# Later modulation columns in a fused encoder block: loads placed behind an attention output's store, products a unit later

## Chip, core and metric

One Trainium2 chip, one of its cores. The metric is device time of one execution, in microseconds (us); the median of three runs of the kernel before is 2392.31 us (2392.06 to 2393.08). All arithmetic that matters here is in 32-bit floats; matrix products are made of three passes over a rounded high part and its remainder.

## What is computed

One encoder layer on 1024 positions of width 1024. Its modulation vector is a small product that is wanted late in the layer:

```python
mod = (silu(c) @ ada_w + ada_b)                 # 1024 x 6144
shift_m, scale_m, gate_m, shift_f, scale_f, gate_f = split(mod, 6)
h = rmsnorm(x, pre_norm_mix) * (1 + scale_m) + shift_m
...                                              # h @ w_in: latents, gates, SSD inputs
y_a = sparse_mla_attention(...) @ w_o_attn       # 16 heads, top 256 keys, biases of relative position
y_b = ssd_mixer(...) @ w_o_ssd
x = x + gate_m * rmsnorm((sig(g_a) * y_a + sig(g_b) * y_b) @ w_out, post_norm_mix)
...                                              # SwiGLU with shift_f, scale_f, gate_f
```

The first 2048 columns of `mod` (shift_m, scale_m) are made at the start by TensorE. The other 4096, in 32 columns of tiles numbered 16 to 47, aren't needed until the attention is over, and are the subject here.

## The kernel before

The layer runs in stages: the normed input and its first projections, the index scores and the choice of keys (to about 668 us), the attention with the last input projections beside it (to about 1145 us), the SSD scan, the output projections, the feed-forward part.

**The attention** is 32 units: 8 pairs of heads (hp), and in each pair the four blocks of 256 queries in the order 0, 2, 1, 3. A call of `attention` weaves two things, unit by unit: the scores of this unit (`att_scores`) and the output of the one before (`att_out`).

- Scores: TensorE forms the query (`puq`, L226), ScalarE and VectorE split it into `qh` and `ql` (L803, L804), TensorE multiplies it with the keys into `plg` (L832). VectorE adds a bias and takes the minimum in one pass (L841); for the near keys the bias is `nm`, which GpSimd has made as the position's bias plus the mask (L816, twice a unit). ScalarE takes the exponential (L844), VectorE the reciprocal `rr` of its sum (L845).
- Output: GpSimd spreads `rr` into `r2` (L852), TensorE transposes the weights (`pt`, L865), ScalarE and VectorE copy them out (`pc`, L870, L868), TensorE multiplies with the values into `po` (L884), VectorE scales into `rb` (L888), and SP stores `rb` to DRAM (L889).

For the first three pairs (12 units) the projections of three last groups of the SSD inputs are woven in, one 128-row product a unit: SP loads weights `wraw` (L150), ScalarE rounds them to `whi` (L151), GpSimd takes the rest `wlo` (L152), TensorE multiplies into a bank `pw` (L236), VectorE convolves and so frees the bank (L961 to L963). `weight_sums` also loads four tiles `wsum` a unit (L997), which VectorE adds (L1002) and SP stores (L1003). In this part TensorE keeps the written order. From the fourth pair on nothing is woven in.

**The later modulation columns.** `ada_next` is called once after each projection (12 times) and once after each unit from the fourth pair on (20 times, and once for the tail). One call makes one column j: `ada_slow` has SP load two tiles `adaw` of 256 KB (L326), GpSimd multiply each by silu(c) (L327) and add the two (L329), and VectorE sum the result into a column of `adas` (L330). There are two `adaw` tiles, so the next column's loads wait until this one's sum is done. After four columns `ada_cols` sums over partitions with four one-column products on TensorE (L296), and VectorE adds the bias into `mod` (L297); it is called at j % 4 == 2.

**What sets the order.** A scheduler with a timeline model of its own places each instruction on its engine; each engine and the SP queue then run strictly in that order. `behind(instruction, first)` forbids the scheduler to place an instruction ahead of another on the same engine; without a second argument, that other one is an early instruction of the start. So before the change the loads, products and additions of a column may stand anywhere after the start.

Of the kernel before, what the change touches and what calls it, by code (L numbers as in the profile page):

```python
# [14 lines left out]
OP = mybir.AluOpType  # L15
AX = mybir.AxisListType

P = 128
# [48 lines left out]
def build(tc, a, dbg=None, stop=99, slots=None):  # L67
    nc = tc.nc
    V, S, G, T, SP = nc.vector, nc.scalar, nc.gpsimd, nc.tensor, nc.sync
# [132 lines left out]
    d_att = dr.tile([KT, P, L], F32, name="d_att")  # L202
# [115 lines left out]
        V.tensor_tensor(mod[:, k:k + 9:8], p[:, 0:2], vec[:, k:k + 9:8], op=OP.add)  # L318
        V.scalar_tensor_tensor(amul[:, k:k + 1], mod[:, 8 + k:9 + k], 1.0, col("pre_mix", k), op0=OP.add, op1=OP.mult)

    def ada_slow(j, acc):

        ts = []
        for h in range(2):
            t = wp.tile([P, 4, P], F32, name="adaw", tag="adaw", bufs=2)
            behind(SP.dma_start(t, a["ada_w"][j - 16][:, 4 * h:4 * h + 4]))  # L326
            behind(G.tensor_tensor(t, t, cs[:, 4 * h:4 * h + 4, None].to_broadcast([P, 4, P]), op=OP.mult))  # L327
            ts.append(t)
        G.tensor_tensor(ts[0], ts[0], ts[1], op=OP.add)  # L329
        V.tensor_reduce(acc, ts[0].rearrange("p k m -> p m k"), axis=AX.X, op=OP.add)  # L330

# [464 lines left out]
    def att_scores(u, uq, nb, out):  # L796

        pq = bank("puq")
        for hh in range(2):
            dense([(pq[:, 256 * hh:256 * hh + 256], u // 2, slice(256 * (u % 2), 256 * (u % 2) + 256))],  # L800
                  [(uq, 2 * hh, [0, 1])], QN)
        qh, ql = Q("qh", dt=F32R), Q("ql", dt=F32R)
        S.activation(qh, pq, AF.Copy, scale=qscale)  # L803
        V.scalar_tensor_tensor(ql, pq, qscale, f(qh), op0=OP.mult, op1=OP.subtract)  # L804
        QQ = (qh, ql)
        rr = sm.tile([P, 4], F32, name="rr", bufs=4)
        out["rr"] = rr
        yield
        for t in range(2):
            i = 2 * u + t  # L810
            n = (i + 1) * P
            near = max(0, n - 256)
            nw = n - near
            nm = Q("nm", (P, 2, 256))
            mk = MK[i][:, near:n] if i in MK else dmask[:, 256 - nw:256]
            G.tensor_tensor(nm[:, :, 0:nw], nb[:, :, 256 - nw:256], mk[:, None, :].to_broadcast([P, 2, nw]), op=OP.add)  # L816
            a_ = max(256, n - 512) if n > 512 else 0
            for hh in range(2):
                st = [QQ[x][:, 256 * hh + 128 * t:256 * hh + 128 * t + 128] for x in range(2)]
                if u >= 2:  # L820
                    lg = R("lg")
                else:
                    if hh == 0:
                        pair = R("lg")
                    lg = pair[:, half(hh)]
                mx = sm.tile([P, 4], F32, name="mx", bufs=6)
                pb_ = {}
                for o_, w_ in ((a_, n - a_),) + (((0, a_),) if a_ else ()):
                    p = bank("plg")
                    w2 = max(w_, 256)  # L830
                    for x, (qi, ki) in enumerate(P3):
                        T.matmul(p[:, 0:w2], st[qi], KVT[ki][:, o_:o_ + w2], start=x == 0, stop=x == 2)  # L832
                    pb_[o_] = p
                parts = [(a_, near, n, nm[:, hh, 0:nw])]
                if near > a_:
                    parts.append((a_, a_, near, MK[i][:, a_:near]))
                if a_:
                    parts.append((0, 0, a_, MK[i][:, 0:a_]))
                m = 3e38
                for x, (o_, s_, e_, add) in enumerate(parts):  # L840
                    V.tensor_tensor_reduce(lg[:, s_:e_], pb_[o_][:, s_ - o_:e_ - o_], add, op0=OP.add, op1=OP.min,  # L841
                                           scale=-1.0, scalar=m, accum_out=mx[:, x:x + 1])
                    m = mx[:, x:x + 1]
                S.activation(lg[:, 0:n], lg[:, 0:n], AF.Exp, scale=-1.0, bias=m, accum_out=mx[:, 3:4])  # L844
                V.reciprocal(rr[:, 2 * t + hh:2 * t + hh + 1], mx[:, 3:4])  # L845
                out[hh, t] = lg
                yield

    def att_out(hp, u, vt, PR):

        r2 = sm.tile([P, 2, 2, 64], F32, name="r2", bufs=1)
        G.tensor_copy(r2, PR["rr"].rearrange("p (t h) -> p t h", t=2)[:, :, :, None].to_broadcast([P, 2, 2, 64]))  # L852
        po = bank("po")
        pov = po[:, 0:256].rearrange("p (t n) -> p t n", t=2)
        last = 2 * u + 1
        parts, copied = {}, []

        def turn(j):
            ts = (0, 1) if j < last else (1,)
            sl = slice(ts[0], 2)  # L860
            pt = (bank if hp < HP_FIRST else bank_d)("pt")
            ptv = pt.rearrange("p (h t n) -> p h t n", h=2, t=2)
            for hh in range(2):
                for t in ts:
                    T.transpose(ptv[:, hh, t, :], PR[hh, t][:, j * P:(j + 1) * P], ident)  # L865
            pc = Q("pc").rearrange("p (h t n) -> p h t n", h=2, t=2)
            if j % 2:
                i = V.tensor_copy(pc[:, :, sl], ptv[:, :, sl])  # L868
            else:
                i = S.activation(pc[:, :, sl], ptv[:, :, sl], AF.Copy)  # L870
            parts[j] = pc, sl
            if hp >= HP_FIRST:
                copied.append(i.ins.name)

        for j in range(last + 1):
            turn(j)
            yield
        after = copied[-1] if copied else None
        for t in range(2):
            behind(T.transpose(po[:, 256 + 128 * t:384 + 128 * t], r2[:, t].rearrange("p h n -> p (h n)"), ident), after)  # L880
        for j in range(last + 1):
            pc, sl = parts.pop(j)
            for hh in range(2):
                behind(T.matmul(pov[64 * hh:64 * hh + 64, sl], vt[:, j, 64 * hh:64 * hh + 64], pc[:, hh, sl],  # L884
                                start=j == 0, stop=j == last, skip_group_check=True), after)
        rb = sm.tile([P, 256], F32, name="rb", bufs=1)
        S.activation(rb, po[:, 256:512], AF.Copy)
        V.tensor_tensor(rb, po[:, 0:256], rb, op=OP.mult)  # L888
        SP.dma_start(d_att[hp][:, 256 * u:256 * u + 256], rb)  # L889
        yield  # L890

    def weave(x, nx, y, ny, z=iter(()), nz=0, lead=1):
# [22 lines left out]
    att = {}  # L915
# [51 lines left out]

    slow, sums = iter(range(16, 48)), {}

    def ada_next():  # L970

        j = next(slow, None)
        if sums and (j is None or j % 4 == 2):
            ada_cols(*sums.popitem())
        if j is not None:
            if j % 4 == 0:
                first[j] = EV("adas", (P, 4, P))
            acc = first[j - j % 4]
            ada_slow(j, acc[:, j % 4])
            if j % 4 == 3:  # L980
                sums[j - 3] = acc

    def group(g):
        return (16 + g, d_bc[g, 0]), (24 + g, d_bc[g, 1]), (2 * g, d_xs[2 * g]), (2 * g + 1, d_xs[2 * g + 1])
# [957 lines left out]
```

## Time and profile before

| what | us |
|---|---|
| median of three runs | 2392.31 |
| the profiled execution, its own time | 2391.81 |
| span of its trace | 2389.7 |
| mean granted TensorE clock | 0.992 of full |
| TensorE busy, of the span | 2329.6 |
| GpSimd (POOL) busy, of the span | 1116.7 |
| attention, first query product to last output's store | 668 to 1144 |
| `adaw` loads: first issue, last issue | 41.0, 1058.1 |
| products with silu(c) (L327): 64, in all | 67.8 |

The page gives busy time by engine, and the costliest groups of instructions with the idle time ahead of them and what ended it. A row of waits says which engine and line waited, for what, how long in all, how often, and the longest. A row of a timeline gives start, duration, engine, line and tile, and in brackets the idle time just before and its releaser. PE is TensorE, DVE is VectorE, ACT is ScalarE, POOL is GpSimd, SPq is SP's queue of DMA issues. Rows of stretches give busy time of each engine in it (PE, PEld, DVE, ACT, POOL, with counts), then the granted clock (PEclk), the DMA share and GB/s.

### The profile page before, as it was taken

The page shows a single profiled execution, that of the slowest core. Times are in us where ns is not written, and L with a number is a line of the kernel's source. Part 1 is how long each engine was busy: PE and PEld are TensorE (multiplying, and loading weights), DVE is VectorE, ACT ScalarE, POOL GpSimd, SP SyncE. Part 2 cuts the span into 40 slices and gives each one's busy share as a digit, 9 for nine tenths or more (in the row PEclk, how much of TensorE's full clock was granted, in tenths as well). Part 3 has the DMA queues.
Part 4 walks back from the last instruction along what each step waited for, and adds up shares of the span by engine and source line. Part 5 has one row for each costly group of instructions (what it writes and reads, how often), then busy time and mean ns, then how long its engine had stood idle before and what let it go on. Part 6 is the DMA issues. An engine that isn't in the chain of part 4 may idle for free. (4 is left out here: it accounts for less than half of the span.)

```text
span 2389.7 us, 35459 instructions
## 1 busy us (share of the span) xinstructions
PE 2329.6 (97%) x11834; PEld 1897.0 (79%) x11834; DVE 1645.0 (69%) x3147; ACT 1266.8 (53%) x2440; POOL 1116.7 (47%) x872
## 2 busy tenths in 40 slices
PE   8999999999999999999999999999999999999997
PEld 6888888888887787777776777788787888888877
DVE  4566775599667676766477878475677877547776
ACT  4456665577455555545677666655564222335452
POOL 3321112222353454652245544778677555544465
PEclk9999999999999999999999999999999999999999
DMA  7123122522235553321588987766475555328664
GB/s 285 62 90 124 63 74 76 163 93 98 92 108 196 171 189 102 102 94 57 186 248 262 313 268 241 239 207 224 134 247 170 178 197 183 114 97 303 219 217 160
DMA packets 245830, 397.13 MB, mean 166 GB/s; under 512 B 24416, under 2 KB 92688, under 8 KB 245648
## 3 DMA queue, kind: packets, MB, share of 16 engines
q1 hardware_dynamic: 244352, 393.25, 49.6%
q8 instruction: 93, 1.52, 0.3%
q10 hardware_dynamic: 1296, 1.63, 0.2%
q14 instruction: 89, 0.73, 0.1%
HBM read 288.33 MB, written 109.60 MB: 167 GB/s over the span
## 5 line engine op out<-in xcount | busy, mean ns | idle before, releaser
L152 POOL TENSOR_TENSOR wlo<-wraw,whi 128x512 fp32r<-128x512 f32 x146 | 198.0, 1357 | 487.2 <-ACT whi L151 445.7
L1551 PE MATMUL p<-xh,wr 128*128 128x512 f32 x880 | 275.7, 391 | 3.8 <-DVE g L1611 2.8
L247 POOL TENSOR_TENSOR wlo<-wraw,whi 128x512 fp32r<-128x512 f32 x119 | 170.7, 1437 | 104.1 <-ACT whi L246 98.9
L1545 POOL TENSOR_TENSOR wr<-a,wr 128x512 fp32r<-128x512 f32 x110 | 159.6, 1460 | 115.0 <-ACT wr L1544 84.5
L1551 PEld LDWEIGHTS p<-xh,wr 128*128 128x128 f32 x880 | 166.0, 189 | 40.0 <-DVE g L1611 3.2
L1551 PE MATMUL p<-xl,wr 128*128 128x512 f32 x440 | 171.9, 391 | 0.0
L151 ACT ACTIVATE whi<-wraw 128x512 fp32r<-128x512 f32 x146 | 91.4, 627 | 131.1 <-issue 47.8
L844 ACT ACTIVATE lg<-lg,mx 128x256 f32<-128x256 f32 (+7 forms) x128 | 98.6, 771 | 104.8 <-DVE mx L841 101.4
L1544 ACT ACTIVATE wr<-a 128x512 fp32r<-128x512 f32 x110 | 68.7, 629 | 141.3 <-PE p L1551 118.2
L1551 PE MATMUL p<-h2h,wr 128*128 128x512 f32 x352 | 111.1, 390 | 0.0
L704 ACT ACTIVATE junk<-acc,cand__2213 128x1024 bf16<-128x1024 f32 (+2 forms) x96 | 86.2, 898 | 45.1 <-DVE cand__2213 L747 29.0
L327 POOL TENSOR_TENSOR adaw<-adaw,cs 128x512 f32<-128x512 f32 x64 | 67.8, 1061 | 88.5 <-DMA adaw<-ada_w 78.6
L246 ACT ACTIVATE whi<-wraw 128x512 fp32r<-128x512 f32 x119 | 74.2, 625 | 59.2 <-PE pos L1346 27.3
L1722 PE MATMUL pfo<-ah,wlo 128*128 128x512 f32 x264 | 103.2, 391 | 2.0 <-POOL wlo L247 2.0
L655 DVE SCALAR_TENSOR_TENSOR acc<-rel,widx,acc 128x384 f32<-128x384 f32 (+2 forms) x90 | 87.0, 987 | 24.7 <-ACT rel L650 24.6
L1722 PE MATMUL pfo<-ah,whi 128*128 128x512 f32 x264 | 103.1, 390 | 0.3 <-ACT whi L246 0.3
L1722 PE MATMUL pfo<-al,whi 128*128 128x512 f32 x264 | 102.8, 389 | 0.0
L650 ACT ACTIVATE rel<-prel 128x512 f32<-128x512 f32 (+3 forms) x160 | 77.2, 523 | 48.3 <-PE prel L649 44.7
L1811 DVE TENSOR_TENSOR al<-al,ah 128x512 fp32r<-128x512 f32 x66 | 73.8, 1120 | 35.8 <-ACT ah L1806 35.6
L1551 PEld LDWEIGHTS p<-xl,wr 128*128 128x128 f32 x440 | 82.9, 188 | 17.1
L702 DVE TENSOR_SCALAR_CACHE_REDUCE junk<-acc,cand__2222 128x896 bf16<-128x896 f32 (+2 forms) x96 | 88.5, 922 | 1.5
L865 PE MATMUL pt<-ident,lg 128*128 128x128 f32 x576 | 83.1, 277 | 5.6 <-ACT pc L870 3.3
(651 smaller groups left out, 7485.4 us busy)
## 6 DMA issues: line engine op xcount, KB each, us to landing
wraw<-w_in SPq DMA_DIRECT2D x130, 256.0 KB, 2.7
a<-w_ffn_in SPq DMA_DIRECT2D x120, 256.0 KB, 3.2
al<-d_a SPq DMA_DIRECT2D x77, 256.0 KB, 3.9
wraw<-w_ffn_out SPq DMA_DIRECT2D x66, 256.0 KB, 3.5
adaw<-ada_w SPq DMA_DIRECT2D x64, 256.0 KB, 2.8
al<-d_ac SPq DMA_DIRECT2D x32, 512.0 KB, 4.8
al<-d_y SPq DMA_DIRECT2D x56, 256.0 KB, 4.2
d_a<-kept SPq DMA_DIRECT2D x33, 256.0 KB, 2.9
```

The lines of the kernel that those rows point to most:

```text
L151: behind(S.activation(hi[:, :kt], raw[:, :kt], AF.Copy))
L152: behind(G.tensor_tensor(lo[:, :kt], raw[:, :kt], f(hi[:, :kt]), op=OP.subtract))
L247: (lo_eng or V).tensor_tensor(lo, src, f(hi), op=OP.subtract)
L650: S.activation(rel[:, 512 * b:512 * b + w_], pr[:, 0:w_], AF.Relu)
L655: V.scalar_tensor_tensor(acc[i][:, 0:n], rel[:, 0:n], ws, acc[i][:, 0:n], op0=OP.mult, op1=OP.add)
L702: V.tensor_scalar(jk, y, a_, 0.0, op0=op, op1=OP.add, accum_out=o)
L704: S.activation(jk, y, AF.Sign, scale=-1.0, bias=a_, accum_out=o)
L844: S.activation(lg[:, 0:n], lg[:, 0:n], AF.Exp, scale=-1.0, bias=m, accum_out=mx[:, 3:4])
L865: T.transpose(ptv[:, hh, t, :], PR[hh, t][:, j * P:(j + 1) * P], ident)
L1545: G.tensor_tensor(w[:, 1], src, f(w[:, 0]), op=OP.subtract)
L1551: T.matmul(p, w[:, wi, i], X[x][i][xi], start=start and i == 0 and k == 0, stop=i == 3 and k == 2, skip_group_check=True)
L1722: T.matmul(o, w[wi][:, P * m:P * m + P], x[xi][:, cl], start=j == 0 and k == 0, stop=j == NP - 1 and k == 2)
```

## The change

One call of `ada_next` is split over two. The loads of column j are issued in one call (`ada_load`), with SP's latest attention store named as what they must stand behind; the products and the sum of that column come in the next call (`ada_fold`), with GpSimd's latest `nm` named as what the products must stand behind. `ada_cols` moves to j % 4 == 3, one call later. The same 64 loads, 64 products, 32 additions, 32 sums and 8 groups of one-column products remain.

```diff
-    def ada_slow(j, acc):
+    def ada_load(j, first):
         ts = []
         for h in range(2):
             t = wp.tile([P, 4, P], F32, name="adaw", tag="adaw", bufs=2)
-            behind(SP.dma_start(t, a["ada_w"][j - 16][:, 4 * h:4 * h + 4]))
-            behind(G.tensor_tensor(t, t, cs[...].to_broadcast([P, 4, P]), op=OP.mult))
+            behind(SP.dma_start(t, a["ada_w"][j - 16][:, 4 * h:4 * h + 4]), first)
             ts.append(t)
+        return ts
+    def ada_fold(ts, acc, first):
+        for h, t in enumerate(ts):
+            behind(G.tensor_tensor(t, t, cs[...].to_broadcast([P, 4, P]), op=OP.mult), first)
         G.tensor_tensor(ts[0], ts[0], ts[1], op=OP.add)
         V.tensor_reduce(acc, ts[0].rearrange("p k m -> p m k"), axis=AX.X, op=OP.add)
...
-            G.tensor_tensor(nm[:, :, 0:nw], ...)
+            att["nm"] = G.tensor_tensor(nm[:, :, 0:nw], ...).ins.name
...
-        SP.dma_start(d_att[hp][:, 256 * u:256 * u + 256], rb)
+        att["stored"] = SP.dma_start(d_att[hp][:, 256 * u:256 * u + 256], rb).ins.name
...
+    loaded = []
     def ada_next():
+        if loaded:
+            j, ts = loaded.pop()
+            if j % 4 == 0:
+                first[j] = EV("adas", (P, 4, P))
+            acc = first[j - j % 4]
+            ada_fold(ts, acc[:, j % 4], att.get("nm"))
+            if j % 4 == 3:
+                sums[j - 3] = acc
         j = next(slow, None)
-        if sums and (j is None or j % 4 == 2):
+        if sums and (j is None or j % 4 == 3):
             ada_cols(*sums.popitem())
         if j is not None:
-            if j % 4 == 0:
-                first[j] = EV("adas", (P, 4, P))
-            acc = first[j - j % 4]
-            ada_slow(j, acc[:, j % 4])
-            if j % 4 == 3:
-                sums[j - 3] = acc
+            loaded.append((j, ada_load(j, att.get("stored"))))
```

What the scheduler makes of it, first on GpSimd, in the eighth unit (second pair, queries 3), where projections are woven in. Before; `nm` are the two masked biases of one unit, `wlo` the remainder of a projection's weights, `r2` the spread reciprocals:

```order
L816 TENSOR_TENSOR nm_7335<-nb_6806,mk_2210 128x512
L327 TENSOR_TENSOR adaw_7999<-adaw_7999,cs_132 128x512
L327 TENSOR_TENSOR adaw_8002<-adaw_8002,cs_132 128x512
L329 TENSOR_TENSOR adaw_7999<-adaw_7999,adaw_8002 128x512
L816 TENSOR_TENSOR nm_7382<-nb_6806,mk_2210 128x512
L327 TENSOR_TENSOR adaw_8209<-adaw_8209,cs_132 128x512
L152 TENSOR_TENSOR wlo_7538<-wraw_7536,whi_7537 128x512
L852 COPY r2_7549<-rr_7274 128x256
```

The same place now (the program is longer, so L816 is L821, L327 is L333, L329 is L334, L852 is L858; numbers of buffers differ):

```order
L821 TENSOR_TENSOR nm_7331<-nb_6802,mk_2210 128x512
L821 TENSOR_TENSOR nm_7378<-nb_6802,mk_2210 128x512
L333 TENSOR_TENSOR adaw_7292<-adaw_7292,cs_132 128x512
L333 TENSOR_TENSOR adaw_7294<-adaw_7294,cs_132 128x512
L334 TENSOR_TENSOR adaw_7292<-adaw_7292,adaw_7294 128x512
L152 TENSOR_TENSOR wlo_7528<-wraw_7526,whi_7527 128x512
L858 COPY r2_7539<-rr_7269 128x256
```

A whole column stood between the unit's two masked biases, and half of the next one ahead of `wlo`; now both biases come first, and one column follows.

GpSimd again, in the sixth pair, queries 2, where nothing is woven in. Before:

```order
L852 COPY r2_9887<-rr_9742 128x256
L327 TENSOR_TENSOR adaw_10648<-adaw_10648,cs_132 128x512
L327 TENSOR_TENSOR adaw_10651<-adaw_10651,cs_132 128x512
L816 TENSOR_TENSOR nm_9897<-nb_9723,mk_2210 128x512
L816 TENSOR_TENSOR nm_9934<-nb_9723,mk_2210 128x512
L329 TENSOR_TENSOR adaw_10648<-adaw_10648,adaw_10651 128x512
```

Now:

```order
L858 COPY r2_9882<-rr_9738 128x256
L821 TENSOR_TENSOR nm_9892<-nb_9719,mk_2210 128x512
L821 TENSOR_TENSOR nm_9929<-nb_9719,mk_2210 128x512
L333 TENSOR_TENSOR adaw_9860<-adaw_9860,cs_132 128x512
L333 TENSOR_TENSOR adaw_9862<-adaw_9862,cs_132 128x512
L334 TENSOR_TENSOR adaw_9860<-adaw_9860,adaw_9862 128x512
```

The products moved from ahead of the biases to behind them; between one unit's `r2` and the next one's, GpSimd now holds the two biases and one column in every unit.

VectorE in that unit, at the store of the output before (L841 is now L847, L845 L851, L888 L894, L804 L809, and the sum L330 is L335). Before:

```order
L841 ISA lg_9951,mx_9952<-plg_9953,nm_9934 128x256
L330 TENSOR_REDUCE adas_10397<-adaw_10648 128x128
L845 RECIPROCAL rr_9886<-mx_9900 128x1
L841 ISA lg_9936,mx_9937<-plg_9942,mk_2210,mx_9937 128x256
L841 ISA lg_9951,mx_9952<-plg_9953,mk_2210,mx_9952 128x256
L845 RECIPROCAL rr_9886<-mx_9915 128x1
L888 TENSOR_TENSOR rb_9972<-po_9889,rb_9972 128x256
```

Now:

```order
L847 ISA lg_9946,mx_9947<-plg_9952,mk_2210,mx_9947 128x256
L335 TENSOR_REDUCE adas_9971<-adaw_9860 128x128
L851 RECIPROCAL rr_9881<-mx_9932 128x1
L894 TENSOR_TENSOR rb_9967<-po_9884,rb_9967 128x256
L851 RECIPROCAL rr_9881<-mx_9947 128x1
L809 SCALAR_TENSOR_TENSOR ql_9994<-puq_9980,qh_9993 128x512
```

The sum of a column stood among the score passes and now stands right ahead of `rb` and of the next unit's `ql`.

On SP's queue one or two columns' loads, anywhere, stood between two attention stores; now from the fourth pair on two loads (one column) follow each store at once, and the next store comes behind them. The columns reach to the last unit, where before the last one was loaded at 1058 us.

More of the change, by code (lines that the diff above doesn't have):

```diff
@@ L325, in ada_slow @@
             t = wp.tile([P, 4, P], F32, name="adaw", tag="adaw", bufs=2)
-            behind(SP.dma_start(t, a["ada_w"][j - 16][:, 4 * h:4 * h + 4]))
-            behind(G.tensor_tensor(t, t, cs[:, 4 * h:4 * h + 4, None].to_broadcast([P, 4, P]), op=OP.mult))
+            behind(SP.dma_start(t, a["ada_w"][j - 16][:, 4 * h:4 * h + 4]), first)
             ts.append(t)
+        return ts
+    def ada_fold(ts, acc, first):
+        for h, t in enumerate(ts):
+            behind(G.tensor_tensor(t, t, cs[:, 4 * h:4 * h + 4, None].to_broadcast([P, 4, P]), op=OP.mult), first)
         G.tensor_tensor(ts[0], ts[0], ts[1], op=OP.add)
@@ L815, in att_scores @@
             mk = MK[i][:, near:n] if i in MK else dmask[:, 256 - nw:256]
-            G.tensor_tensor(nm[:, :, 0:nw], nb[:, :, 256 - nw:256], mk[:, None, :].to_broadcast([P, 2, nw]), op=OP.add)
+            att["nm"] = G.tensor_tensor(nm[:, :, 0:nw], nb[:, :, 256 - nw:256], mk[:, None, :].to_broadcast([P, 2, nw]),
+                                        op=OP.add).ins.name
             a_ = max(256, n - 512) if n > 512 else 0
@@ L968, in build @@
     slow, sums = iter(range(16, 48)), {}
+    loaded = []
     def ada_next():
-        j = next(slow, None)
-        if sums and (j is None or j % 4 == 2):
-            ada_cols(*sums.popitem())
-        if j is not None:
+        if loaded:
+            j, ts = loaded.pop()
             if j % 4 == 0:
@@ L978, in ada_next @@
             acc = first[j - j % 4]
-            ada_slow(j, acc[:, j % 4])
+            ada_fold(ts, acc[:, j % 4], att.get("nm"))
             if j % 4 == 3:
                 sums[j - 3] = acc
+        j = next(slow, None)
+        if sums and (j is None or j % 4 == 3):
+            ada_cols(*sums.popitem())
+        if j is not None:
+            loaded.append((j, ada_load(j, att.get("stored"))))
     def group(g):
```

## The prediction

> **What bounds the kernel now.** I read the page first, then the waits of the attention (670 to 1150 us), since every moved instruction lies in it, then the timelines at the largest waits, and last a stretch of the same loop in which no column is made.
>
> ```profile
> span 2389.7 us, 35459 instructions
> ...
> PE 2329.6 (97%) x11834; PEld 1897.0 (79%) x11834; DVE 1645.0 (69%) x3147; ACT 1266.8 (53%) x2440; POOL 1116.7 (47%) x872
> ```
>
> TensorE is busy in 97% of the span. So nothing that GpSimd or SP does counts unless TensorE stops for it. TensorE's stops in the attention, from the view of waits cut to TensorE and to 670 to 1150 us:
>
> ```profile
> PE plg L832 <- DVE mx L841: 7.4, 9, 2.1
> PE pw L236 <- DVE cv L962: 5.3, 2, 4.1
> PE pt L865 <- ACT pc L870: 3.3, 4, 1.7
> PE pt L865 <- ACT lg L844: 1.6, 3, 0.9
> PE plg L832 <- DVE ql L804: 1.2, 2, 0.9
> PE plg L832 <- DVE rb L888: 1.1, 1, 1.1
> PE pt L865 <- DVE pc L868: 0.5, 1, 0.5
> ```
>
> That is 20.4 us, mostly put down to VectorE. What VectorE and GpSimd themselves wait for in the same 480 us:
>
> ```profile
> POOL adaw L327 <- DMA adaw<-ada_w: 76.0, 42, 4.9
> ...
> DVE adas L330 <- POOL adaw L329: 14.9, 10, 4.5
> DVE lg L841 <- POOL nm L816: 14.4, 11, 2.5
> ```
>
> GpSimd stands 76.0 us with a column's product at its head, waiting for the load, and what is queued behind it waits too: the masked bias `nm` comes late 11 times and the column's sum 10 times, which holds VectorE 29.3 us. The reader is to see the chain load, product, bias, score pass, TensorE, and that only its last link is paid for.
>
> The two places where it shows best. Around 800 us, second pair, queries 3 (VectorE, then GpSimd, then SP):
>
> ```profile
> 799.13 0.42 DVE L841 CUSTOM_DVE_ANT_0 lg<-plg,nm 128x256 f32<-128x256 f32 x1 [2.31 <-POOL nm L816]
> ...
> 809.50 0.80 DVE L1002 TENSOR_TENSOR wsum<-wsum 128x512 f32<-128x512 f32 x1 [2.02 <-DMA wsum<-w_o_ssd]
> ```
>
> ```profile
> 797.94 1.15 POOL L816 TENSOR_TENSOR nm<-nb,mk 128x512 f32<-128x512 f32 x1
> 801.16 1.04 POOL L327 TENSOR_TENSOR adaw<-adaw,cs 128x512 f32<-128x512 f32 x1 [2.06 <-PE pw L236]
> 802.16 1.28 POOL L152 TENSOR_TENSOR wlo<-wraw,whi 128x512 fp32r<-128x512 f32 x1
> ```
>
> ```profile
> 803.46 0.33 SPq L150 DMA_DIRECT2D wraw<-w_in  x1
> 803.89 1.81 SPq L997 DMA_DIRECT2D wsum<-w_o_ssd  x4
> ```
>
> The second `nm` runs behind a column and is 2.31 us late. Then GpSimd idles 2.06 us for the next column's product, `wlo` runs only behind that, SP's load of `wraw` waits for `wlo`'s end (803.44 us) to have its buffer, and the loads of `wsum` queue behind it, so VectorE waits another 2.02 us. Both delays, 4.33 us together, are column work, and they are the 4.1 us of the wait `pw <- cv` (the other one, 1.2 us, is a unit of the third pair of the same shape).
>
> Around 1020 us, sixth pair, queries 2:
>
> ```profile
> 1020.45 2.04 POOL L327 TENSOR_TENSOR adaw<-adaw,cs 128x512 f32<-128x512 f32 x2 [3.32 <-DMA adaw<-ada_w]
> 1022.45 2.26 POOL L816 TENSOR_TENSOR nm<-nb,mk 128x512 f32<-128x512 f32 x2
> ```
>
> ```profile
> 1023.63 0.42 DVE L841 CUSTOM_DVE_ANT_0 lg<-plg,nm 128x256 f32<-128x256 f32 x1 [2.54 <-POOL nm L816]
> ```
>
> GpSimd waits 3.32 us for the load, runs both products and only then the biases; VectorE loses 2.54 us.
>
> The counter-check, TensorE's waits between 1067.5 and 1133 us, where the same loop runs without columns:
>
> ```profile
> PE plg L832 <- DVE rb L888: 1.1, 1, 1.1
> PE plg L832 <- DVE mx L841: 0.7, 3, 0.3
> ```
>
> The 1.1 is the end of the last column (the wait ended at 1067.16). What is left is 0.7 us in 65.5 us. A unit there lasts about 10 us, so a unit that isn't disturbed loses 0.1 us.
>
> **The change, part by part.** *Biases ahead of the products.* In every unit both `nm` now precede the column, so the wait that a load causes on GpSimd can't reach them. Of TensorE's waits I take as caused by columns: 7.4 (`plg <- mx`), 5.3 (`pw <- cv`), 1.1 (`plg <- rb`), 0.5 (`pt <- pc` of VectorE), and of the 3.3 behind ScalarE's `pc` an estimate of 1.0, 15.3 us in all; nothing at all of the 1.6 and 1.2. What stays is the undisturbed rate, 0.1 us in each of 32 units, 3 us. Gain 12.3 us, bounded by 15.3 above, and below by half of it, 7.6 us, if each stop only goes over to the next cause.
>
> *The granted clock.* Stops cost twice here:
>
> ```profile
> 810.00:820.00 10.00, 9.51 (x39) 7.87 (x40) 6.05 (x16) 3.65 (x5) 0.00 (x0) 0.83 0.57 199
> 890.00:900.00 10.00, 8.73 (x53) 7.01 (x50) 5.59 (x14) 7.17 (x12) 6.23 (x6) 0.83 0.43 129
> 1000.00:1010.00 10.00, 8.67 (x53) 6.94 (x54) 8.03 (x31) 5.63 (x11) 6.07 (x7) 0.83 0.36 118
> 1020.00:1030.00 10.00, 7.96 (x44) 6.27 (x44) 6.96 (x30) 3.50 (x9) 6.55 (x6) 0.83 0.38 125
> ```
>
> Four stretches of 10 us have a mean clock of 0.83; each comes right behind a stop and costs 0.17 x 10 = 1.7 us of matmul work, 6.8 us together. I take three of the four as saved, 5.1 us (between 1.7 and 6.8), since one stop that stays can still bring one.
>
> The Trainium skill, page "TensorE: Matmul & The Clock Gate", section "Why this matters for your kernels", puts the limit at idle gaps of about 3 us. By that rule only the 4.1 us stop would have lowered the clock, and the term would be 1.7 instead of 5.1 us. The trace disagrees: no other stop is over 2.1 us, and three more drops are there.
>
> *Loads behind the store, sums behind the loads.* The rows of a column, and two stores in the stretch without columns:
>
> ```profile
> L327 POOL TENSOR_TENSOR adaw<-adaw,cs x64: 1039/1041/1492, 56.0 to 1063.1; 128x512 f32<-128x512 f32 x64
> L329 POOL TENSOR_TENSOR adaw<-adaw x32: 1266/1288/1703, 58.2 to 1064.4; 128x512 f32<-128x512 f32 x32
> L330 DVE TENSOR_REDUCE adas<-adaw x32: 1034/1072/1111, 682.1 to 1065.7; 128x128 f32<-128x512 f32 x32
> ...
> DMA to landing us min/median/max: 2.4/2.8/6.6
> ```
>
> ```profile
> 1105.81 0.32 SPq L889 DMA_DIRECT2D d_att<-rb  x1
> ```
>
> ```profile
> 1113.71 10.54 SPq L889 DMA_DIRECT2D d_att<-rb  x2
> ```
>
> On SP a row of two merged loads or stores takes at least 0.32 us an issue, and I allow 0.43 us from issue to issue (1.81 us for four, above). The second load is then issued 0.86 us behind the store, lands 2.8 us later (3.66), its product ends at 4.7, the addition at about 6.1 us, and the sum can start. It stands right ahead of the next `rb`, a store interval later. The shortest interval is that of a small unit: 7.90 us here, from which `rb` with its store (about 0.5) and the sum itself (1.07) go off: 6.3 us of room against 6.1. The next one is 10.2 us (the merged row holds two stores, 0.32 us the last: 1113.71 + 10.54 - 0.32 = 1123.93), with 2.6 us of room. So VectorE waits at the sum by tenths, in five small units: 5 x 0.3 = 1.5 us at most half of which reaches TensorE. GpSimd waits for the load still, up to 4 us a unit, but behind that wait stand only this column, `r2` (wanted at the unit's end) and in the first three pairs `wlo`. Eight columns move into the stretch that had none, 8 x 1.07 us on VectorE, which is two thirds busy; 1 us of it shows. With the 0.86 us a unit that two issues hold SP ahead of `vt`, `uraw` and `nb`, which are wanted a unit later (0), I put the new costs at 3 us, between 0 and 8.
>
> *One-column products a call later.* Eight groups of four small products and eight additions: as many as before, on the same two engines, 0. The scheduler also shuffles some SSD and output instructions behind 1145 us; no row says which way that goes: 0, between -2 and 2 us.
>
> *Sum:* 12.3 + 5.1 - 3 = 14.4 us. The profiled execution took 2391.81 us (2.1 us more than its span), so 2377.4; it lies 0.5 us under the median of 2392.31. Forecast for the median: 2378 us.
>
> **The rivals.** *The stop goes over to another engine.* VectorE also waits for ScalarE's exponentials, ahead of `rr`:
>
> ```profile
> DVE rr L845 <- ACT lg L844: 35.9, 50, 1.8
> ```
>
> If these 35.9 us, or a `wsum` that is late for other reasons than at 809.50, take the place of the columns, half of the 15.3 us stays, and with it all drops of the clock but one: 7.6 + 1.7 - 3 = 6 us less 2 for the shuffle: 2388. Against it: without columns TensorE lost 0.7 us in 65.5 with the same ScalarE.
>
> *The clock drops anyway.* If the drops go by where a stop falls in time more than by its length, as the mix of 1.2 and 4.1 us stops that got one suggests, new ones take the place of the old: 12.3 - 3 = 9.3 us, 2382.5. This is beside the skill's rule above, which by a smaller term points the same way.
>
> *Late products hold VectorE (slower).* The sum now stands ahead of `rb` and of `ql`, with TensorE's next `plg` waiting for `ql`. Where it did so before:
>
> ```profile
> 1065.74 1.03 DVE L330 TENSOR_REDUCE adas<-adaw 128x128 f32<-128x512 f32 x1 [4.50 <-POOL adaw L329]
> ```
>
> VectorE lost 4.50 us and TensorE 1.1, a quarter. Landings reach 6.6 us. One at that figure comes 3.8 us late, past the 2.6 us of room in an ordinary unit and past all in a small one, so it decides from about 5.4 us on. If most of 20 units land so late, at 1.5 us each (between a quarter and a half of 3.8) for 12 of them, that is 18 us, against the 8 us that the first three pairs still gain (5.3 + 3.4 less what stays): 2392 + 18 - 8 = 2402. For it: each column's room is a single store interval. Against it: the median of 2.8 us, and that a later store moves the next one too.
>
> That the change doesn't reach its aim at all, because the scheduler puts the instructions elsewhere, is excluded by the order shown: both biases precede the products in every unit.
>
> **How the numbers follow.** Forecast 0.62, stop goes over 0.17, clock drops anyway 0.08, late products 0.13. A measurement of this kernel can tell 0.2% (4.8 us) from no change. Forecast and clock case lie under 2387.5: faster 0.70. The stop that goes over is within: same 0.17. Slower 0.13. The range begins at 2369, where all 15.3 + 6.8 us go and nothing new comes (2370) with a little of the shuffle, and goes to 2391, which takes in the first two rivals and leaves out the slower one.
>
> **What would show it.** Right: `lg <- nm` nearly gone from VectorE's waits (14.4 before), TensorE's waits of the attention at 5 to 8 instead of 20.4 us, at most one or two stretches with a clock under 1, the last attention store at about 1130 instead of 1144 us, the rest of the span as long as before. GpSimd's wait for the loads may stay at some 70 us. Wrong: `adas <- adaw` over 20 us with TensorE waiting at `ql` or `rb` (late products), or `pw <- cv` still there with `wsum` or ScalarE ahead of it (goes over), or stretches at 0.83 with no stop over 1 us ahead (clock).

## The result, and the profile after

The changed kernel takes 2375.57 us (median of six runs, 2373.03 to 2379.5), the kernel before beside it 2392.18 (2389.73 to 2393.22): a ratio of 0.9931, with a 95% interval of 0.9921 to 0.9942. Timed a second time on another occasion the pair gave 2379.34 and 2395.85 us, a ratio of 0.9928 (0.9913 to 0.9942). So the change gains 0.7%, about 16.5 us. The medians themselves wandered by 4 to 5 us from one occasion to the next, so below a kernel is compared by its ratio to the kernel before that ran beside it.

The profiled execution of the changed kernel took 2375.33 us. Its span with the same 11834 matmuls, and TensorE's waits between 670 and 1150 us, where 20.4 us stood before:

```profile
span 2373.5 us, 35401 instructions
...
PE 2323.9 (98%) x11834; PEld 1895.7 (80%) x11834; DVE 1647.2 (69%) x3147; ACT 1266.3 (53%) x2440; POOL 1114.8 (47%) x872
```

```profile
PE plg L838 <- DVE ql L809: 3.6, 2, 1.9
PE pw L236 <- DVE cv L968: 1.9, 1, 1.9
PE plg L838 <- ACT pc L876: 1.5, 1, 1.5
PE pt L871 <- ACT lg L850: 1.5, 2, 1.0
PE plg L838 <- DVE mx L847: 1.2, 5, 0.2
PE pt L871 <- ACT pc L876: 0.5, 1, 0.5
```

The score pass (`mx`) has gone from 7.4 us to 1.2, and the sum is 10.2 us. But `ql` has risen from 1.2 to 3.6, and a `cv` wait is still there. VectorE and GpSimd in the same stretch:

```profile
DVE adas L335 <- POOL adaw L334: 9.8, 9, 3.4
...
DVE wsum L1013 <- DMA wsum<-w_o_ssd: 5.7, 4, 2.1
...
POOL adaw L333 <- DMA adaw<-ada_w: 74.7, 26, 8.5
```

VectorE's wait for `nm` (14.4 us) no longer appears as a row of its own. GpSimd still waits 74.7 us for loads, almost as long as the 76.0 before: the same wait, and it now costs nothing there. The reader should take from this pair that a wait on an engine has no price until one knows what is queued behind it.

The attention's last store, from the timeline of SP, stood at 1143.86 us before:

```profile
1127.69 0.34 SPq L895 DMA_DIRECT2D d_att<-rb  x1
```

That is 16.2 us earlier, exactly the 16.2 us by which the span is shorter. To see where in the attention they come from, the span is cut at the first `puq` of the first, the fourth and the eighth pair of heads (timeline of TensorE). This cut is used for all kernels below; the columns of a row add up to the span.

| kernel (profiled execution), us | ahead | first three pairs (woven) | pairs 4 to 7 | eighth pair to the end | span |
|---|---|---|---|---|---|
| before | 668.3 | 248.3 | 176.7 | 1296.4 | 2389.7 |
| changed | 667.6 | 246.4 | 162.0 | 1297.5 | 2373.5 |
| changed, second profile | 669.2 | 246.3 | 162.0 | 1299.2 | 2376.7 |
| 1: products behind the biases | 669.7 | 247.0 | 162.7 | 1300.1 | 2379.5 |
| 2: loads behind the store | 667.6 | 244.5 | 161.8 | 1303.5 | 2377.4 |
| 3: a third tile | 671.7 | 244.8 | 176.2 | 1294.8 | 2387.5 |
| 4: changed, loads free | 668.4 | 249.4 | 161.8 | 1297.0 | 2376.6 |
| 5: before, loads doubled | 668.9 | 264.8 | 188.2 | 1307.3 | 2429.2 |
| 6: changed, loads doubled | 669.3 | 248.3 | 182.4 | 1311.1 | 2411.1 |
| 7: changed, no later columns | 667.7 | 236.7 | 158.5 | 1298.7 | 2361.6 |
| 8: changed, weight sums later | 667.4 | 241.4 | 162.8 | 1304.5 | 2376.1 |
| 9: changed, no weight additions | 667.7 | 237.7 | 161.7 | 1302.2 | 2369.3 |
| 10: weight sums later, loads free | 671.7 | 241.5 | 163.7 | 1299.4 | 2376.3 |
| 11: no columns in the woven pairs | 668.3 | 236.9 | 160.9 | 1356.9 | 2423.0 |

The change is worth 14.7 us in pairs 4 to 7, where nothing is woven in, and only 1.9 us in the first three. A row shows one execution; those of runs 2, 3 and 4 took 5.2, 5.7 and 7.0 us less than their medians, so for these the row doesn't show where the median's time lies.

### The profile page after: what moved, and what is told of

It is laid out like the page before. It is cut to its first block, busy times and chain, and to the rows that moved or that the text cites. A ratio compares the mean times of both kernels' runs of the same rounds, so it can differ in the third digit from the quotient of the medians.

```text
span 2373.5 us, 35401 instructions
## 1 busy us (share of the span) xinstructions
PE 2323.9 (98%) x11834; PEld 1895.7 (80%) x11834; DVE 1647.2 (69%) x3147; ACT 1266.3 (53%) x2440; POOL 1114.8 (47%) x872
## 5 line engine op out<-in xcount | busy, mean ns | idle before, releaser
L333 POOL TENSOR_TENSOR adaw<-adaw,cs 128x512 f32<-128x512 f32 x64 | 67.4, 1071 | 74.8 <-DMA adaw<-ada_w 74.7
L1357 PE MATMUL pos<-ah,whi 128*128 128x512 f32 x216 | 84.9, 393 | 0.5 <-ACT whi L246 0.5
```

What stands on the lines that cost most here:

```text
L1357: T.matmul(p, w[wi][:, q], xs[k][xi], start=n in "1532AB" and h == 0 and q == 0 and x == 0, stop=h == 1 and q == 3 and x == 2, skip_group_ ...
```

## Experiments

Theory N: a product that stands ahead of `nm` on GpSimd makes the biases late, and the order of these two is the gain. Rival S: the placing of the loads is the gain. Theory W (and its opposite V) is on what is left in the woven pairs.

### 1. The kernel before, products behind the biases

```diff
-            behind(G.tensor_tensor(t, t, cs[...], op=OP.mult))
+            behind(G.tensor_tensor(t, t, cs[...], op=OP.mult), att.get("nm"))
```

> The kernel before, with one thing of the change: a column's products stand behind both biases nm of the unit. Loads are placed freely and the column is still made in one call. Theory N (GpSimd's wait for a column's load ahead of nm was the cause): VectorE's wait for nm falls from 14.4 to under 3 us, TensorE's waits of the attention from 20.4 to 9 to 12 us, and the time to 2376 to 2382 us, 10 us or more of the change's 16.6. Theory S (the spacing of the loads behind a store and a call of room for them is what counts): GpSimd's wait for loads and VectorE's waits behind it only go over from nm to the sums; 2388 us or more.

Measured: 2381.26 us, ratio 0.9938 (0.9923 to 0.9953). GpSimd's waits between 667 and 1146 us:

```profile
POOL adaw L327 <- DMA adaw<-ada_w: 2.4, 3, 1.9
```

VectorE's wait for `nm` is gone, TensorE's waits are 12.1 us. Pairs 4 to 7 take 162.7 us, against 162.0 with the whole change. This one argument is enough for nearly all of the gain in these pairs, with the loads placed freely: theory N there. The loads land long before the product is due, and that gains no more than with 74.7 us of waiting.

### 2. The kernel before, loads behind the store

```diff
-            behind(SP.dma_start(t, a["ada_w"][j - 16][...]))
+            behind(SP.dma_start(t, a["ada_w"][j - 16][...]), att.get("stored"))
```

> The kernel before, with the other thing of the change: a column's loads stand behind the latest output store; the products follow in the same call and are free to stand ahead of nm. Theory N: nm still comes late behind products that wait for loads, VectorE's wait for nm stays at 10 us or more, and the time at 2387 to 2396 us. Theory S: 2376 to 2382 us.

Measured: 2384.43 us, ratio 0.9947 (0.9931 to 0.9963). By the time alone this is rival S. But the edit didn't leave the order alone, as GpSimd's timeline shows (the first two rows are a small unit, the others an ordinary one):

```profile
960.17 1.04 POOL L327 TENSOR_TENSOR adaw<-adaw,cs 128x512 f32<-128x512 f32 x1 [1.67 <-DMA adaw<-ada_w]
961.17 1.16 POOL L816 TENSOR_TENSOR nm<-nb,dmask 128x512 f32<-128x512 f32 x1
...
976.39 2.29 POOL L816 TENSOR_TENSOR nm<-nb,mk 128x512 f32<-128x512 f32 x2
979.14 2.04 POOL L327 TENSOR_TENSOR adaw<-adaw,cs 128x512 f32<-128x512 f32 x2 [0.47 <-DMA adaw<-ada_w]
```

In pairs 4 to 7 the scheduler, with the load behind the store, puts both products behind both biases by itself in 13 of 16 units; only three small units keep a product between them. VectorE's wait for `nm` is down to 6.7 us (8 times). So the two halves of the change aren't independent: in these pairs each brings nearly the same order about, and this run can't tell N from S. Runs 3 to 6 were made for that. In the woven pairs it is the other way: all ten units with a column have both products ahead of the second bias (before, six units had), and yet these pairs take 244.5 us, less than before (248.3) and than with the whole change (246.4). So N doesn't carry over to them.

### 3. The kernel before with a third `adaw` tile

```diff
-            t = wp.tile([P, 4, P], F32, name="adaw", tag="adaw", bufs=2)
+            t = wp.tile([P, 4, P], F32, name="adaw", tag="adaw", bufs=3)
```

> The kernel before with three adaw tiles instead of two, so that one of a column's two loads can be issued a column earlier; products may still stand ahead of nm. Theory N, as a wait for loads: GpSimd's wait for loads falls from 76 to under 40 us, VectorE's wait for nm from 14.4 to under 8 us, and the time by 5 to 10 us. Theory N2 (the work of the products ahead of nm delays it, 1.0 to 3.5 us a unit, wait or not): under 4 us gained.

Measured: 2395.04 us, ratio 0.9995 (0.9984 to 1.0005), no gain. GpSimd's wait for loads did fall, from 76.0 to 56.6 us, and VectorE's wait for `nm` from 14.4 to 6.5, yet TensorE's waits stayed (19.8 us) and so did pairs 4 to 7 (176.2). The largest stop in them, from the timeline of all engines:

```profile
999.27 1.04 POOL L327 TENSOR_TENSOR adaw<-adaw,cs 128x512 f32<-128x512 f32 x1 [1.17 <-DMA adaw<-ada_w]
1000.27 1.29 POOL L168 TENSOR_TENSOR ul<-uraw,uh 128x512 fp32r<-128x512 f32 x1
1001.51 1.04 POOL L327 TENSOR_TENSOR adaw<-adaw,cs 128x512 f32<-128x512 f32 x1
1002.51 2.26 POOL L816 TENSOR_TENSOR nm<-nb,mk 128x512 f32<-128x512 f32 x2
1003.70 0.42 DVE L841 CUSTOM_DVE_ANT_0 lg<-plg,nm 128x256 f32<-128x256 f32 x1 [2.75 <-POOL nm L816]
```

Here the load accounts for 1.17 us. The rest of the lateness is work: two products of 1.04 us and the query weights' remainder ahead of the biases. TensorE stops for 3.02 us behind it. So the products' own work counts too (N2 in the expectation), which neither the prediction nor the first form of N said. But the order didn't stay the same either: in pairs 4 to 7 GpSimd now has 13 products ahead of a unit's second bias, in 8 units of 16, where it had 9 in 6 (counted in its timeline from one `r2` to the next). What the run shows is that less waiting buys nothing while products stand ahead of the biases; it doesn't separate the wait from the work.

### 4. The changed kernel, loads free

```diff
-            behind(SP.dma_start(t, a["ada_w"][j - 16][...]), first)
+            behind(SP.dma_start(t, a["ada_w"][j - 16][...]))
```

> The changed kernel with its loads placed freely again; the products stay a call later and behind nm. Theory N (the biases ahead of the products are the gain): GpSimd no longer waits for loads (under 10 us instead of 74.7), VectorE's wait for late sums (9.8 us) goes, and the time is the same as the changed kernel's within 3 us. Theory S (loads behind the store are needed, since early ones get in the way of SP's other transfers): 4 us or more slower than the changed kernel, with TensorE's waits of the attention at 15 us or more.

Measured: 2385.69 us, ratio 0.995 (0.9934 to 0.9965), beside 0.9928 (0.9913 to 0.9942) for the changed kernel on the same occasion. The intervals overlap a little, so that it is slower is likely, not certain. By the medians it is 6.4 us slower, which is S's forecast and not N's (the same within 3 us); TensorE's waits, 14.1 us, are just under S's 15. In the profiled execution, pairs 4 to 7 are as fast (161.8), with GpSimd's wait at 8.4 instead of 73.0 us: S is wrong there. In the woven pairs it is 3.1 us slower. SP's queue shows what the store's place is good for:

```profile
SPq L326 <- POOL adaw L334: 101.7, 23, 6.4
...
SPq L326 <- DVE rr L851: 57.6, 16, 11.3
SPq L326 <- DVE adas L335: 35.8, 13, 7.3
```

Without the constraint a load stands at the head of SP's queue until what frees its tile is done, 195 us in all, and the loads of `wsum` queue behind it: VectorE's wait for `wsum` is 11.7 us against 6.1, TensorE's behind `ql` 7.4 against 3.4. So S has a part in the woven pairs, by the mechanism that this run's expectation names. How large it is stays open: this execution took 2378.72 us, no more than the changed kernel's profiled one beside it (2378.60), so the 6.4 us between the medians lie in executions that no trace shows.

### 5 and 6. Every load twice, before and changed

```diff
             behind(SP.dma_start(t, a["ada_w"][j - 16][...]), ...)
+            behind(SP.dma_start(t, a["ada_w"][j - 16][...]), ...)
```

> The kernel before with every load of a later column issued twice, the same data into the same tile, so that a product waits longer for its load. Theory N: where products stand ahead of nm the longer wait reaches VectorE and TensorE; about 30 columns by some 2 us more at GpSimd, a quarter to a half of it paid: 15 to 30 us slower than before. Theory T (GpSimd's wait is mostly slack, and the gain came from the new order of something else): under 5 us slower.

> The changed kernel with every load of a later column issued twice, as in the run beside it. Theory N: behind the waiting products stands nothing that is wanted soon, so GpSimd waits longer (over 100 us) and TensorE hardly: 0 to 5 us slower than the changed kernel. Theory T or late products (the sum ahead of ql and rb): 10 us or more slower, with VectorE's wait for the sums over 30 us.

Measured: before with doubled loads 2431.41 us, ratio 1.0154 (1.0136 to 1.0171); changed with doubled loads 2413.25, ratio 1.0076 (1.006 to 1.0091). That is 35.6 us slower than before and 33.9 us slower than the changed kernel. The first was expected at 15 to 30, the second at 0 to 5: theory N in its simple form fails on the second run. VectorE's waits, first of the kernel before, then of the changed one:

```profile
DVE lg L842 <- POOL nm L817: 30.8, 17, 4.7
...
DVE adas L331 <- POOL adaw L330: 23.5, 14, 5.3
```

```profile
DVE adas L336 <- POOL adaw L335: 65.0, 22, 5.8
```

Before, a late load hits `nm` (14.4 to 30.8 us). After, it hits the column's sum (10 to 65 us), which stands on VectorE ahead of `rb` (and `nm` for 6.9 us). And `rb` is what the store sends, behind which the next loads stand. One turn of that ring, from the changed kernel's timeline with doubled loads:

```profile
1045.24 0.33 SPq L896 DMA_DIRECT2D d_att<-rb  x1
1045.68 0.87 SPq L326 DMA_DIRECT2D adaw<-ada_w  x2
...
1048.49 0.33 SPq L327 DMA_DIRECT2D adaw<-ada_w  x1
...
1049.58 0.33 SPq L327 DMA_DIRECT2D adaw<-ada_w  x1
...
1052.41 1.04 POOL L334 TENSOR_TENSOR adaw<-adaw,cs 128x512 f32<-128x512 f32 x1 [3.51 <-DMA adaw<-ada_w]
...
1054.81 1.28 POOL L335 TENSOR_TENSOR adaw<-adaw 128x512 f32<-128x512 f32 x1
1056.13 1.07 DVE L336 TENSOR_REDUCE adas<-adaw 128x128 f32<-128x512 f32 x1 [2.44 <-POOL adaw L335]
...
1057.18 0.41 DVE L895 TENSOR_TENSOR rb<-po,rb 128x256 f32<-128x256 f32 x1
1057.62 0.33 SPq L896 DMA_DIRECT2D d_att<-rb  x1
```

The second copies go into the same tiles and are issued only at 1048.49 and 1049.58 us, when the first have landed. Store, loads, product, addition, sum, `rb`, store: 12.38 us, and the unit lasts 13.3 us (first `puq` to first `puq`) where it lasts 11.8 without doubling. Against the changed kernel's second profile, pairs 4 to 7, with units of about 10 us, lose 20.4 us; the woven pairs, with units of about 20 us, lose 2.0. In the kernel before both lose (11.5 and 16.5). Another 11.9 us come from the eighth pair on, 9.7 of them before the last store, in units that stand in the same ring. So the change closed a ring that a unit must be long enough for. It fits as it is, with little to spare: as an estimate from the changed kernel's rows, the second product starts 4.9 us behind a store (median of pairs 4 to 7), and product, addition, sum and `rb` make it some 8.7 us, against stores that are 9.1 us apart or more. That the ring sets the pace, and not the later sum alone, is read from this one turn; with doubled loads the stores are 6.8 to 14.1 us apart.

### 7. The changed kernel without later columns

```diff
-    slow, sums = iter(range(16, 48)), {}
+    slow, sums = iter(()), {}
+    V.tensor_copy(mod[:, 16:48], col("ada_b", 16, 32))
```

> The changed kernel without later columns: no loads, products, sums nor one-column products of columns 16 to 47, whose part of mod is the bias alone. It shows what is left of the columns' price. Theory N: what the columns still cost is VectorE's 32 sums of 1.07 us, mostly beside TensorE's work: 2369 to 2375 us, under 7 us less than the changed kernel. Theory R (columns still hold the woven part up, through wlo and the loads of wsum): TensorE's waits in the first three pairs go too, 2360 to 2367 us.

Measured: 2364.52 us, ratio 0.9874 (0.986 to 0.9888). Against the changed kernel's 0.9928 the columns still cost some 13 us: the change took a little over half of their price. Of what is left 9.7 us lie in the woven pairs (246.4 to 236.7) and 3.5 in pairs 4 to 7. Theory R is right: TensorE's waits of the attention are 5.0 us, with neither `cv` nor `wsum` behind them.

```profile
PE pt L871 <- ACT pc L876: 2.2, 2, 1.7
PE plg L838 <- DVE mx L847: 1.9, 9, 0.2
PE pt L871 <- ACT lg L850: 0.7, 2, 0.5
PE plg L838 <- DVE ql L809: 0.2, 1, 0.2
```

### 8 and 9. The weight sums in the woven pairs

The two stops of the changed kernel that a drop of the clock follows, from its timeline:

```profile
807.03 1.46 DVE L1013 TENSOR_TENSOR wsum<-wsum 128x512 f32<-128x512 f32 x1 [1.13 <-DMA wraw<-w_in]
...
809.21 0.86 DVE L1013 TENSOR_TENSOR wsum<-wsum 128x512 f32<-128x512 f32 x1
...
809.99 0.68 DVE L809 SCALAR_TENSOR_TENSOR ql<-puq,qh 128x512 fp32r<-128x512 f32 x1
...
810.72 0.50 PE L838 MATMUL plg<-kvth,ql 128*128 128x512 f32 x1 [1.86 <-DVE ql L809]
...
832.05 0.69 DVE L1013 TENSOR_TENSOR wsum<-wsum 128x512 f32<-128x512 f32 x1 [0.86 <-DMA wsum<-w_o_ssd]
832.66 0.22 DVE L968 SCALAR_TENSOR_TENSOR cv<-pw,vec,cv 128x3 f32<-128x3 f32 x1
...
832.93 0.79 PE L236 MATMUL pw<-h0h,whi 128*128 128x512 f32 x1 [1.95 <-DVE cv L968]
```

In both the addition of a weight sum stands on VectorE ahead of what TensorE waits for. Run 8 puts the additions a call later and behind `ql`; run 9 leaves them out, so that the unsummed tiles are stored.

```diff
 def weight_sums():
+    if taken:
+        weight_adds(*taken.pop())
...
+def weight_adds(m, h, ts):
...
-    V.tensor_tensor(o, x, y, op=op)
+    behind(V.tensor_tensor(o, x, y, op=op), att["ql"])
```

> The changed kernel, with the four additions of the weight sums put a call later than their loads and behind the unit's ql. Theory W (what TensorE still loses in the three woven pairs comes from VectorE standing at a late wsum ahead of the convolution and of ql): VectorE's wait for wsum falls from 5.7 to under 1 us, the waits plg behind ql (3.6) and pw behind cv (1.9) go, and with them one or both of the two stretches at a clock of 0.83; 2368 to 2372 us. Theory V (the late load only hides another late one, ScalarE's or the rounding of the weights): within 1.5 us of 2375.6 with the same stops at another releaser.

> The changed kernel with the four additions of each weight sum left out: the loaded tiles are stored as they are, so later products use other weights. Of VectorE's work 32 additions of 0.6 to 0.8 us go. Theory W: 2367 to 2372 us, as with the additions put later, or a little less for the 0.7 us each that VectorE no longer works. Theory V: 2374 us or more.

Measured: run 8 2377.23 us, ratio 0.9923 (0.9907 to 0.9939); run 9 2372.56, ratio 0.9907 (0.989 to 0.9924). The woven pairs give 5.0 and 8.7 us, so W is right on the place: in run 8 the waits behind `wsum` and `ql` are gone. On the time it isn't: run 8's ratio lies within the changed kernel's interval, nearer to what V had, and run 9's 2372.56 us lies between the two. One stop stayed there:

```profile
PE pw L236 <- DVE cv L968: 1.9, 1, 1.9
PE plg L838 <- DVE mx L847: 1.5, 6, 0.3
```

At that place (827.63 us) the convolution now starts late behind ScalarE, whose last `whi` stands ahead of the convolution's first pass, as V had it. And little of the 5.0 us reaches the end: from the eighth pair on, run 8 takes 7.0 us more than the changed kernel. TensorE's waits behind 1128 us are 23.5 instead of 20.5 and what the clock loses from 1150 us to the last matmul 8.5 instead of 6.8 us, 4.7 of the 7.0; the rest isn't seen in these views. Runs 2 and 9 have the same (6.0 and 4.7 us). In runs 1, 2, 6, 8, 9 and 10 the scan's instructions stand in another order than in the changed kernel, and the stretch from the last attention store to the end takes 1248.1 to 1251.8 us. In the kernel before, the changed kernel (both profiles) and runs 3 and 4, which have nearly one order there, it takes 1244.3 to 1247.3. So the order that an edit of the attention leaves behind it goes with up to 6 us. That it is the cause isn't shown: runs 5 and 7, with nearly the changed kernel's order, take 1249.2 and 1249.0.

### 10. Both: loads free, weight sums later

Its edits are those of runs 4 and 8.

> The changed kernel with loads placed freely and the additions of the weight sums a call later behind ql. If what TensorE still loses has two sources, late columns and late weight sums, this takes both: attention 3 to 6 us shorter, 2370 to 2374 us. If what the attention gains is given back behind it, as with the weight sums alone, within 2 us of the changed kernel.

Measured: 2378.22 us, ratio 0.9928 (0.9914 to 0.9941), the same as the changed kernel. The woven pairs keep the 5 us of run 8 (241.5), and the gain doesn't show at the end. Beside the changed kernel's second profile it is lost ahead of the attention (2.5 us) and in pairs 4 to 7 (1.7), not behind the attention as the expectation had it; two profiles of one kernel differ by 1.6 us ahead of the attention, so most of this is not clear of the spread.

### The changed kernel again

> The changed kernel once more, for comparison with the three below on the same chip: about 2376 us by every theory, and the two medians of the changed kernel tell how far medians of this kernel wander.

Its 2379.34 us are 3.8 us over the first median, with the kernel before 3.7 us over its own: the two ratios agree within 0.0003.

### 11. No columns in the woven pairs

```diff
                 convolved(ch, dst, p)
-                ada_next()
```

> The changed kernel with no columns in the first three pairs: the twelve calls behind the projections go, so columns begin with the fourth pair and the last twelve are made behind the attention, beside the SSD scan. Theory R (what columns still cost lies in the woven pairs, where they make the loads of wsum and the last convolution late): second and third pair as without columns, 81 to 82 us each instead of 87 and 85.5, so 8 to 9 us gained there. Behind the attention twelve columns are added, 12.8 us of VectorE's work: if TensorE hides it, 2368 to 2372 us, faster than both kernels; if VectorE or the loads hold the scan up, the gain is given back there: 2375 us or more.

Measured: 2424.86 us, ratio 1.0119 (1.0102 to 1.0137), 27.7 us slower than before. The first half came out as forecast: the woven pairs take 236.9 us, what they take without any columns. The twelve columns behind the attention cost six times that. TensorE's waits between 1100 and 1500 us, and then the stretch right behind the attention (us, PE, PEld, DVE, ACT, POOL, clock, DMA share, GB/s), where the changed kernel has TensorE busy for all of 100 us:

```profile
PE adap L296 <- DVE adas L335: 17.3, 6, 9.2
PE pyd L1124 <- DVE al L1085: 12.9, 5, 5.1
PE pyd L1124 <- DVE X L1093: 6.3, 2, 3.8
```

```profile
1130.00:1230.00 100.00, 64.48 (x310) 47.97 (x309) 62.95 (x84) 47.37 (x109) 63.69 (x55) 0.83 0.65 203
```

VectorE is hardly busier there (62.95 us of 100) than in the changed kernel (62.17), so VectorE's work isn't the price: the one-column products stand in TensorE's order and wait there for a column that isn't ready, up to 9.2 us at a time. That is 17.3 us. Another 19.2 us TensorE waits for the scan's `al` and `X`, while VectorE itself waits 15.9 us for late sums of columns (1118 to 1240 us). The clock takes 22.2 instead of 6.8 us from 1150 us to the last matmul. A moved step that ends on the bound engine takes its latency along.

## Why the prediction was right, point by point

**The time.** 2378 us was forecast, 2375.57 measured, inside the range. As a profile, 14.4 us were forecast and the span lost 16.2. The agreement is closer than the terms are: the gaps and the clock came out 3.8 us short together, the 3 us of new costs hardly came, and at least 2.6 of the 16.2 us are in no term of the sum. So part of the agreement is luck.

**TensorE's gaps.** Forecast 12.3 us, and 20.4 to 10.2 measured, 10.2 us. The sign "5 to 8" for what stays was missed. The mechanism (product, bias, score pass, TensorE) is shown for pairs 4 to 7 by runs 1, 2 and 4 together: the biases come first in all three (in run 2 in 13 of 16 units), GpSimd's wait for loads in the attention is 2.4, 88.3 and 8.4 us, and the pairs take 161.8 to 162.7. But the two halves of the sum were off in opposite directions. In pairs 4 to 7 TensorE's waits fell from 12.5 to 2.5 us (first the largest row before, then all rows of the changed kernel):

```profile
PE plg L832 <- DVE mx L841: 7.2, 8, 2.1
```

```profile
PE plg L838 <- ACT pc L876: 1.5, 1, 1.5
PE plg L838 <- DVE mx L847: 1.0, 4, 0.2
```

That is about the undisturbed rate, as forecast, and with the clock's two drops there (3.4 us) it makes 13.4 of the 14.7 us. In the woven pairs the forecast was "the 8 us that the first three pairs still gain", and 1.9 came.

**The step that failed.** "Both delays, 4.33 us together, are column work." Columns do cause the stop (without them it goes, run 7), but biases ahead of products don't cure it. In run 1, with no product ahead of a bias, it is still there, behind a wait of VectorE of 2.54 us for `wsum`:

```profile
PE pw L236 <- DVE cv L962: 3.0, 1, 3.0
```

In the changed kernel three stops of 1.70, 1.86 and 1.95 us (748.94, 810.72 and 832.93 us), each behind an addition of `wsum`, stand against three before of 0.9, 4.1 and 1.3 us (727, 810 and 895 us); TensorE's waits in the woven pairs fell only from 6.5 to 5.5 us. By which way a column makes `wsum` late (its loads, its products ahead of `wlo`, or its place in SP's queue) no run separates. This is the first rival, "the stop goes over to another engine", true in the woven pairs alone; `pw <- cv` with `wsum` ahead of it was named as its sign.

**The clock.** Three of four drops were taken as saved, 5.1 us; there are two fewer, 3.4 us. The two of pairs 4 to 7 went. The woven pairs have two as before, now behind two `wsum` stops: one at the same place, one new at 832.93 us for the one at 890. Where the stops went, the drops went, so the rival "drops anyway" didn't decide here. It isn't excluded: one and the same stop of 1.5 us behind `pc`, at the start of pair 4, stands in both profiles of the changed kernel and in runs 4, 8, 9 and 10, and in run 10 alone a drop follows it.

**New costs.** 3 us were allowed. In pairs 4 to 7 the columns still cost 3.5 us (run 7), but that isn't this term: TensorE waits 2.5 us there with columns and 3.4 without, and its 40 one-column products keep it busy for 4.8 us, which the prediction counted as unchanged work. What shows of the new costs is 1.1 us in the eighth pair, into which columns moved. The shuffle behind the attention was put between -2 and 2; from the last store to the end both kernels take 1245.8 us. The other edits, run 11 aside, moved that by -1.5 to 6.0 us, so that bound was too narrow and held by luck.

**Late products.** VectorE's wait for late sums fell from 14.9 to 9.8 us, so the slower rival didn't come. Its mechanism is real: run 6 shows that the sum ahead of `rb` takes over the price once a column's two products start 6.5 and 8.4 us behind the store instead of 3.9 and 4.9 (medians of pairs 4 to 7). The forecast price, 1.5 us a unit, is near what came, 20.4/16 = 1.3.

**What the reasoning lacked.** It put the lateness down to the wait for loads. Run 3 shows that the products' own work ahead of the biases counts too, and the first two runs that in pairs 4 to 7 either half of the change brings nearly the same order about.

## What to carry to other kernels

Price a wait by what is queued behind it: GpSimd stood 75 us for loads before and after, and what changed the time, in pairs 4 to 7, was whether the biases stood behind the products. When a step is tied to a store and the store to a result that stands behind the step, count the ring once around and compare it with the shortest unit; here doubling the loads cost 34 us. And where a scheduler orders by its own model, look at the order that an edit brought about before reading its time: run 2 said "the loads matter" by its time and, in pairs 4 to 7, "the order" by its rows.

## What the runs showed of the hardware

What length of stop lowers the granted clock. Between 660 and 1150 us of all fourteen profiles TensorE stopped 26 times for 1.86 us or more, and a stretch of 5 us with a clock under 0.99 lies at or right behind 23 of them (the other three, of 2.04 to 2.08 us, are in runs 4 and 6). Of 53 stops of 0.9 to 1.83 us six were followed by a drop, the shortest of 1.00 us. In the changed kernel the 1.70 us stop at 748.94 us left the clock at 1.00, and this is the stretch behind the one of 1.95 us at 832.93 us:

```profile
830.00:840.00 10.00, 8.05 (x40) 6.67 (x39) 7.16 (x15) 5.52 (x8) 4.15 (x4) 0.83 0.87 301
```

The Trainium skill, page "TensorE: Matmul & The Clock Gate", section "Why this matters for your kernels", speaks of idle gaps of over about 3 us. Here the measurement differs: most stops from 1.86 us on, far fewer below, and the length alone doesn't decide.
